# A hybrid attention layer whose residual gate moves from TensorE to VectorE, with the entry of the softmax attention and the planner's costs rewritten

## The chip, the core and the metric

The kernel runs on one core of a Trainium2 chip. The metric is device time in microseconds, the median of several executions; one further execution is recorded by the hardware profiler. A measurement of this kernel can tell a difference of about 0.3% from none.

## What is computed

One layer over 1024 latent tokens and 256 context tokens of width 1024. Two branches read the same modulated input: a bidirectional chunked gated linear attention (GLA, 4 heads) and a differential softmax attention (8 heads, two score maps each). Their outputs are merged and projected, and the residual gate `g_x` scales the result:

```python
mod_x = jax.nn.silu(c) @ w_ada[layer] + b_ada[layer]
sh_x, sc_x, g_x = jnp.split(mod_x[:, None, :], 3, axis=-1)
pl = project(modulate(x, sh_x, sc_x), w_in[layer])
pc = project(modulate(ctx, sh_c, sc_c), w_in[layer])
...
o_gla = bidir_gla(q, k, v, la_f, la_b, s_f, s_b)
...
o_diff = diff_attention(q1, q2, concat(ck1, k1), concat(ck2, k2), concat(cv, dv), lam)
a = merge_heads(rms_norm(o_gla) * gla_gain) * silu(gla_gate)
b = merge_heads(rms_norm(o_diff) * diff_gain * (1 - lam_init)) * silu(diff_gate)
y = sigmoid(m_gla) * (a @ w_br_gla) + sigmoid(m_diff) * (b @ w_br_diff)
x = x + g_x * (y @ w_out[layer])
```

`g_x` is one row of 1024 numbers: the last third of `silu(c) @ w_ada + b_ada`.

## The kernel before

All data are fp32. A product of accuracy near fp32 is made of three one-pass products (`mm3`, L322): each operand is split into a rounded part and a rest (`split`, L332: ScalarE copies, VectorE subtracts).

The program is written as many small generators, and a planner (`Driver`, L57) decides at build time in which order TensorE, ScalarE, VectorE and GpSimd get their instructions. It keeps a clock of its own, with a cost for each instruction (`Engine`, L175, and `mm`, L316) and for each transfer (`Driver.dma`, L118), and at each moment issues what is due, by priority. On the chip the engines do not look at that clock: each takes its instructions strictly in the order so written, and waits where an input is late. So a change of the costs changes the order and nothing else. Transfers all stand in one queue on SP, in order too.

The work goes in three phases.

- Phase A (`phase_a`, L752): fifteen jobs stream slices of `w_in` through three load buffers (tag `raw`), split them (tag `w`), and multiply (PSUM tag `mm`) for keys, values, queries and gates; what later phases need is stored in DRAM (`d_kT`, `d_dv`, `d_qT`, ...). Into the second half of this stream the planner weaves the GLA's four heads (PSUM tags `gs`, `go`, `gt`; `gla_head`, L1046), whose small products depend on one another.
- The residual gate (`job_gate`, L702) is made in phase A. Its slice of `w_ada` is loaded and split like any weight, and 32 products with the two parts of `silu(c)` (`cs`) as stationary operand give two rows of 512 columns twice, which go to DRAM (`d_g`). In phase C `gate` (L1839) loads them back to all partitions and adds bias.
- Phase B (`phase_b`, L1755) is the attention. It begins when the stream and the GLA are both done (`ev_b2`, `ev_b`). `att_keys`, `att_queries` and `att_values` (L1336 to L1370) load the operands (tags `kk`, `aq`, `vv`). For each head and each tile of 128 queries TensorE makes scores (tags `st` for 256 and `s2` for 1024 keys), VectorE the maximum, ScalarE the exponentials, VectorE the difference of the two maps (tag `e5`); TensorE transposes the result in groups of 4, 4 and 2 (`att_tr`, L1466, PSUM tag `b1`), ScalarE copies each group from PSUM (tag `ac`), GpSimd splits it (tags `at4`, `at2`), and for each pair of tiles TensorE multiplies with the values (`att_av`, L1491, also PSUM tag `b1`, of which there are two). `att_fin` (L1548) normalises, with two more transposes from tag `b1k`. Between all this `fill` (L1599) gives TensorE other products (tags `mb`, `wt`), one half tile per 1.3 query tiles.
- Phase C (`phase_c`, L1813): the merge and the output product (tag `mc`).

Of the kernel before, what the change touches and what calls it, by code (L numbers as in the profile page):

```python
# [56 lines left out]
class Driver:  # L57
# [60 lines left out]
    def dma(self, nbytes, dst, src):  # L118
        t = max(self.free["DGE"], self.now, self.ready.get(self.key(src), 0.0)) + 0.6
        self.free["DGE"] = t  # L120
        t = max(self.free["DMA"], t + 0.6) + nbytes / 360e3
        self.free["DMA"] = t
        t += 1.8
        k = self.key(dst)
        self.ready[k] = max(t, self.ready.get(k, 0.0))
        return At(t)
# [48 lines left out]
class Engine:  # L175
# [5 lines left out]
    def __getattr__(self, what):  # L181
        f = getattr(self.eng, what)

        def emit(out, *args, **kw):
# [8 lines left out]
            psum = any(x.space == PSUM for x in ins)  # L193
            if self.name == "ACT":
                c = 0.06 + 0.000833 * n + 0.093 * scalars + (0.0 if psum else 0.04)
            elif self.name == "DVE":
                fast = what in ("tensor_scalar", "tensor_copy") and not psum
                c = 0.07 + n / 960 * (0.5 if fast else 2.0 if "scan" in what else 8.0 if what == "reciprocal" else 1.0)
            elif ALU.pow in args:
                c = 0.3 + 0.165 * n  # L200
            elif what == "tensor_tensor":
                c = 0.15 + 0.0021 * n
            else:
                c = 0.16 + 0.00083 * n + 0.083 * scalars
# [9 lines left out]
class Hybrid:  # L214

    TAGS = dict(
        h=("sb", 32), raw=("sb", 3), sm=("sb", 32),
# [10 lines left out]
        wt=("sbW", 4), ft=("sbW", 2), aq=("sbB2", 4), kk=("sbB2", 3), vv=("sbB2", 3),  # L228
        e5=("sbB", 6), at4=("sbB", 6), at2=("sbB", 2), ac=("sbB", 2), b1k=("sbB", 5), fin=(None, 2),

        yy=("sbC", 32), o=("sbC", 4), gb=("sbC", 1), wx=("sbC", 4),

        mm=("psA", 3), tp=("psA", 2), gs=("psA1", 1), go=("psA1", 1), gt=("psA1", 1),
        mb=("psW", 1), s2=("psB", 2), st=("psB1", 1), b1=("psB1", 2), mc=("psC", 4),
    )
    POOLS = dict(sb="left", sbA="left", sbB="left", sbC="left",
# [99 lines left out]


    def build(self):
        tc = self.tc
        with (  # L340
# [4 lines left out]
            with tc.manual_schedule(engines={ENG.PE, ENG.Activation, ENG.DVE, ENG.Pool}):  # L345
                self.open("sb", "sbA", "psA", "psA1", "sbA1")
# [4 lines left out]
                self.close("psC", "psW", "sbW", "sbC", "sb")  # L351

    def scratch(self):
# [14 lines left out]
        self.d_g = d("d_g", [2, D])  # L368
# [383 lines left out]
    def phase_a(self):  # L752
# [8 lines left out]
        self.ev_st = {(nm, c, i): Event() for nm in ("gg", "dq", "dg") for c in range(2) for i in range(8)}  # L761
# [29 lines left out]
        def stream():  # L791
            for n, j in enumerate(jobs):
# [6 lines left out]
                if n == self.NG:  # L799
                    d.spawn(self.job_gate(), prio=8)  # L800
# [176 lines left out]
    def post_qk(self, isk, c, i, pm):  # L977
# [37 lines left out]
        for j in range(4):  # L1015
# [10 lines left out]
                   ("pl", 2), ev=None if isk else self.ev_st["dq", c, i])  # L1026
# [343 lines left out]
    def att_values(self):  # L1370
        yield self.ev_b2
# [227 lines left out]
    def fill(self):  # L1599
# [8 lines left out]
        yield self.ev_b2  # L1608
# [12 lines left out]
        def conv(n, raw):  # L1621
            tg = wtag(n)
            if tg == "wx":
# [11 lines left out]

        d.spawn(load(), prio=3)
# [274 lines left out]
```

## Time and profile before

| | us |
|---|---|
| median of 3 runs | 1765.09 (1763.59 to 1769.03) |
| the profiled execution, device time | 1769.03 |
| its span in the profile | 1767.3 |
| TensorE busy | 1703.3 (96%) |
| VectorE busy | 1056.0 (60%) |
| ScalarE busy | 761.1 (43%) |
| GpSimd busy | 735.4 (42%) |

The profile gives one execution. A row names an engine, an operation, the tile written and those read (`out<-in`, without numbers), how often it stands there and how long it took. PE is TensorE's matmul, PEld its weight load, DVE is VectorE, ACT is ScalarE, POOL is GpSimd, SP the queue of transfers. The ends of matmuls are modelled, since they overlap: 128x512 matmuls are listed with some 0.4 us each and follow one another faster than that. A number in square brackets behind a row is idle time before it, with what ended it.

### The profile page before, as it was taken

Reading aid. Unit: us, or ns where it says so; the run is one execution under the profiler, and the core shown is the slowest. Engines: PE = TensorE matmul, PEld = TensorE weight load, DVE = VectorE, ACT = ScalarE, POOL = GpSimd, SP = SyncE. Lnnn points to the kernel's source line nnn. Section 1 sums busy time; section 2 is a strip of 40 time slices with the busy share of each in tenths; the row PEclk is TensorE's granted clock in tenths of the full one; section 3 lists DMA queues with packets and bytes.
Section 4 is the critical chain, followed back from the end, with each engine's and each line's share of the span. In section 5 each row is a group of like instructions: output and inputs, shape, how many; then the busy total and the mean of one; then the engine's idle time right before and its main releaser. Section 6 shows DMA issues by size and latency. Waiting matters only on the chain.

```text
span 1767.3 us, 25056 instructions
## 1 busy us (share of the span) xinstructions
PE 1703.3 (96%) x8633; PEld 1400.0 (79%) x8633; DVE 1056.0 (60%) x1895; ACT 761.1 (43%) x1759; POOL 735.4 (42%) x918
## 2 busy tenths in 40 slices
PE   7999999999999999999999999999999898999998
PEld 3788768888888788788788788788887787888887
DVE  4535233615553768878852987777877788535532
ACT  4546342212242444443432666566665555522200
POOL 1500001403333445545530577777876776831000
PEclk9999999999999999999999999999999999999999
DMA  8423352433743545555447344345348553269522
GB/s 310 146 81 133 129 179 90 131 123 118 220 147 113 187 144 171 149 154 168 132 131 190 91 121 124 107 114 133 113 114 251 176 143 96 81 201 303 180 102 84
DMA packets 244903, 259.90 MB, mean 147 GB/s; under 512 B 20860, under 2 KB 176420, under 8 KB 244776
## 3 DMA queue, kind: packets, MB, share of 16 engines
q1 hardware_dynamic: 244776, 258.30, 47.9%
q8 instruction: 68, 1.11, 0.3%
q14 instruction: 59, 0.48, 0.1%
HBM read 171.72 MB, written 86.52 MB: 146 GB/s over the span
## 4 chain that ended last, share of the span: by engine, by line
PE 78%; DVE 12%; ACT 3%; DMA 3%; issue 2%; POOL 2%; SPq 0%; ACTq 0%; DVEq 0%; POOLq 0%
PE mm L317 38%; PE mc L317 12%; PE mb L317 7%; DVE sm L185 6%; PE b L317 4%; PE s L317 4%; PE b L329 3%; PE go L317 3%; PE gs L317 2%; PE st L317 2%; PE tp L329 2%; PE gt L317 2%; DVE e L185 1%; POOL sm L185 1%; DVE b1k L185 1%
## 5 line engine op out<-in xcount | busy, mean ns | idle before, releaser
L317 PE MATMUL mm<-w,h 128*128 128x512 f32 x2304 | 570.6, 399 | 0.9 <-ACT w L185 0.7
L317 PEld LDWEIGHTS mm<-w,h 128*128 128x128 f32 x2304 | 425.7, 188 | 86.9 <-ACT w L185 1.1
L185 POOL TENSOR_TENSOR at<-ac,at 128x512 fp32r<-128x512 f32 (+1 forms) x192 | 237.5, 1237 | 16.0
L317 PE MATMUL mb<-h,wt 128*128 128x512 f32 x792 | 213.7, 406 | 5.6 <-DVE ft L185 5.4
L185 POOL TENSOR_SCALAR sm<-sm 128x1 f32<-128x1 f32 (+1 forms) x78 | 17.8, 228 | 458.1 <-DVE sm L185 343.7
L185 POOL TENSOR_SCALAR at<-ac 128x512 fp32r<-128x512 f32 (+1 forms) x192 | 136.0, 708 | 168.1 <-ACT ac L185 167.3
L185 DVE TENSOR_TENSOR w<-raw,w 128x512 fp32r<-128x512 f32 x136 | 97.6, 737 | 116.7 <-ACT w L185 113.1
L317 PEld LDWEIGHTS mb<-h,wt 128*128 128x128 f32 x792 | 140.2, 189 | 31.5 <-DVE ft L185 6.1
L185 ACT ACTIVATE p<-mm 128x512 f32<-128x512 f32 (+1 forms) x116 | 67.5, 587 | 217.5 <-PE mm L317 199.7
L185 ACT ACTIVATE ac<-b 128x512 f32<-128x512 f32 (+1 forms) x213 | 107.5, 511 | 122.3 <-PE b L329 101.7
L185 DVE TENSOR_REDUCE sm<-s 128x1 f32<-128x1024 f32 x128 | 155.6, 1216 | 2.7 <-PE s L317 1.5
L185 ACT ACTIVATE e<-s,sm 128x1024 f32<-128x1024 f32 x128 | 143.9, 1124 | 0.0
L317 PE MATMUL b<-at,vv 128*128 128x256 f32 x960 | 130.1, 288 | 10.0 <-ACT ac L185 7.2
L317 PE MATMUL mm<-h,w 128*128 128x512 f32 x576 | 139.1, 398 | 0.5 <-DVE h L185 0.4
L317 PEld LDWEIGHTS b<-at,vv 128*128 128x128 f32 x960 | 122.4, 193 | 16.6 <-ACT ac L185 9.8
L317 PE MATMUL s<-kk,aq 128*128 128x512 f32 x512 | 133.6, 398 | 0.3 <-ACT p L185 0.3
L317 PEld LDWEIGHTS mm<-h,w 128*128 128x128 f32 x576 | 108.9, 191 | 25.4 <-DVE h L185 1.1
L185 POOL TENSOR_TENSOR sm<-sm,nhalf 128x1 f32<-128x1 f32 (+2 forms) x110 | 115.7, 1052 | 31.2 <-DVE sm L185 21.9
L317 PEld LDWEIGHTS s<-kk,aq 128*128 128x128 f32 x512 | 91.7, 191 | 15.6 <-ACT p L185 0.5
L185 DVE SCALAR_TENSOR_TENSOR e<-e,sm,e 128x1280 f32<-128x1280 f32 x64 | 102.3, 1598 | 0.1
L185 ACT ACTIVATE w<-raw 128x512 fp32r<-128x512 f32 x136 | 82.0, 625 | 40.6 <-PE mm L317 24.9
L329 PE MATMUL b<-ident,e 128*128 128x128 f32 x604 | 94.0, 277 | 5.0 <-ACT ac L185 4.5
(195 smaller groups left out, 2647.3 us busy)
## 6 DMA issues: line engine op xcount, KB each, us to landing
raw<-in_w_in SPq DMA_DIRECT2D x72, 512.0 KB, 4.2
aq<-d_qT SPq DMA_DIRECT2D x128, 128.0 KB, 3.4
d_kT<-pl SPq DMA_DIRECT2D x40, 256.0 KB, 2.3
d_dv<-pl SPq DMA_DIRECT2D x40, 256.0 KB, 2.2
gv<-d_v SPq DMA_DIRECT2D x40, 256.0 KB, 3.1
kk<-d_kT SPq DMA_DIRECT2D x32, 320.0 KB, 6.3
vv<-d_dv SPq DMA_DIRECT2D x16, 640.0 KB, 6.1
d_aT<-gpl SPq DMA_DIRECT2D x64, 128.0 KB, 2.1
```

What stands on the lines that cost most here:

```text
L185: f(out, *args, **kw)
L317: self.nc.tensor.matmul(out, lhsT, rhs, start=start, stop=stop)
L329: self.nc.tensor.transpose(out, src, self.ident[:n, :n])
```

## The change

Three things.

The gate: `job_gate` loads the slice of `w_ada` in the same pieces, and VectorE multiplies each by the column `silu(c)` per partition and adds up over the eight pieces into `gb`. One product with a matrix of ones then sums over the partitions, for each of the two halves, which leaves the gate on all partitions at once; VectorE adds the bias, GpSimd halves it. The trip through DRAM and `gate` in phase C go away.

The entry of the attention: the buffers of the keys (`kk`) move to a pool that is there from the start, so the first keys load as soon as they have been stored (`ev_st["dk", ...]`). The values wait for the first queries. `fill` loads its first weights after the last of phase A's, not at the end of the GLA.

The planner's costs: new numbers for transfers, ScalarE, VectorE, GpSimd and TensorE. The order of all four engines comes out anew. The buffers of dynamic transfers shrink (`dynamic_dma_scratch_size`), and an unused tile `edge` of 96 bytes sets where the pools begin.

```diff
     def dma(self, nbytes, dst, src):
-        t = max(self.free["DGE"], self.now, self.ready.get(self.key(src), 0.0)) + 0.6
+        t = max(self.free["DGE"], self.now, self.ready.get(self.key(src), 0.0)) + 0.45
...
+            acc = "accum_out" in kw
+            scalars -= acc and n > 1
             if self.name == "ACT":
-                c = 0.06 + 0.000833 * n + 0.093 * scalars + (0.0 if psum else 0.04)
+                c = 0.2 + 0.000833 * n + 0.093 * scalars - (0.028 if psum else 0.0) + (0.21 if acc else 0.0)
             elif self.name == "DVE":
                 fast = what in ("tensor_scalar", "tensor_copy") and not psum
-                c = 0.07 + n / 960 * (0.5 if fast else 2.0 if "scan" in what else 8.0 if what == "reciprocal" else 1.0)
+                c = 0.16 + 0.055 * scalars + n * 0.00104 * (
+                    0.5 if fast else 2.0 if "scan" in what else 8.0 if what == "reciprocal" else 1.0)
...
-        c = (max(n, 256) if rhs.dtype == F32R else 2 * max(2 * n, 256)) / 2400
+        c = 0.009 + max(n, 230) * 0.000428 if rhs.dtype == F32R else 0.006 + max(4 * n, 470) / 2400
...
     def job_gate(self):
         yield self.ev_la
-        wd = self.wstream([(self.a["w_ada"][0], 2048), (self.a["w_ada"][0], 2560)], "w", prio=2)
+        a = self.a
+        gb = self.gb = self.t("gb", [P, 2, 512])
         for n in range(2):
+            o = 2048 + n * 512
+            for kk in range(NK // 2):
+                yield from self.acq("raw")
+                raw = self.t("raw", [P, 2, 512])
+                self.dma(raw, a["w_ada"][0][kk * 256:(kk + 1) * 256, o:o + 512].rearrange("(k p) c -> p k c", p=P))
+                yield self.d.when(raw)
+                for j in range(2):
+                    k = 2 * kk + j
+                    c = self.col[:, k:k + 1]
+                    if k == 0:
+                        e = self.dve.tensor_scalar(gb[:, n], raw[:, j], c, None, ALU.mult)
+                    else:
+                        e = self.dve.scalar_tensor_tensor(gb[:, n], raw[:, j], c, gb[:, n], ALU.mult, ALU.add)
+                    yield e
+                self.rel("raw", e)
+            yield from self.acq("p")
+            bias = self.t("p", [P, 512])
+            self.dma(bias, a["b_ada"][0:1, o:o + 512].to_broadcast([P, 512]))
             yield from self.acq("gs")
-            pm = self.t("gs", [2, 512])
-            for k in range(NK):
-                yield wd[n, k]
-                wh, wl = wd[n, k].w
-
-                prods = [(pm, self.cs[:, k, ::2], wh), (pm[:1], self.cs[:, k, :1], wl)][::-1 if k else 1]
-                for x, (o, c, w) in enumerate(prods):
-                    e = self.mm(o, c, w, k == 0 and x == 0, k == NK - 1 and x == 1)
-                self.rel("w", e, 2)
-                yield AtPE(0)
-            yield from self.acq("p")
-            st = self.t("p", [2, 512])
-            self.rel("gs", self.act.activation(st, pm, AF.Copy))
-            self.store([(self.d_g[:, n * 512:(n + 1) * 512], st)], ("p", 1))
+            pm = self.t("gs", [P, 512])
+            yield self.d.whenpe(gb)
+            e = self.mm(pm, self.ones, gb[:, n], True, True)
+            yield e
+            yield self.d.when(bias)
+            e = self.dve.tensor_tensor(bias, pm, bias, ALU.add)
+            self.rel("gs", e)
+            yield e
+            self.rel("p", self.pool.tensor_scalar(gb[:, n], bias, 0.5, 0.0, ALU.mult, ALU.add))
...
-                    d.spawn(self.job_gate(), prio=8)
+                    d.spawn(self.job_gate(), prio=2)
...
     def att_keys(self):
-        yield self.ev_b2
+
         for hd in range(8):
             c, x = hd // 4, hd % 4
+            for i in range(10):
+                yield self.ev_st["dk", c, i]
+            if hd:
+                yield self.ev_q[0, 1]
...
     def att_values(self):
-        yield self.ev_b2
+        yield self.ev_q[0, 0]
...
-        yield self.ev_b2
...
         def conv(n, raw):
             tg = wtag(n)
+            yield self.ev_b2
...
+        yield self.wload[-1]
         d.spawn(load(), prio=3)
```

How the order moves, at three places. First TensorE where the gate's products stand (tile `gs`, read from `w` and `cs` before). Before:

```order
L317 MATMUL mm_2032<-h_567,w_2002 128x512
L317 MATMUL gs_1784<-w_2074,cs 1x512
L317 MATMUL gs_1784<-w_2073,cs 2x512
L317 MATMUL gs_1784<-w_2090,cs 1x512
L317 MATMUL gs_1784<-w_2089,cs 2x512
L317 MATMUL gs_1784<-w_2094,cs 1x512
L317 MATMUL gs_1784<-w_2093,cs 2x512
L317 MATMUL gs_2118<-w_2099,cs 2x512
L317 MATMUL gs_2118<-w_2100,cs 1x512
```

and now:

```order
L320 MATMUL mm_2139<-h_365,w_1982 128x512
L320 MATMUL mm_2139<-h_366,w_1982 128x512
L320 MATMUL mm_2139<-h_365,w_1983 128x512
L320 MATMUL gs_2152<-gb_1816,ones 128x512
L320 MATMUL mm_2139<-h_562,w_1992 128x512
L320 MATMUL mm_2139<-h_563,w_1992 128x512
```

Of 32 products, of which 22 stood together with nothing between them, two are left, each among the matmuls of a job.

Second, SP at the entry of the attention, behind the last two stores of the GLA (`d_aT`). Before:

```order
L282 DMA d_aT_95<-gpl_8552 128x2x128
L282 DMA d_aT_99<-gpl_8553 128x2x128
L282 DMA d_m_117<-p_8565 128x512
L282 DMA kk_8597<-d_kT_88 64x1280
L282 DMA kk_8597<-d_kT_90 64x1280
...
L282 DMA kk_8603<-d_kT_90 64x1280
L282 DMA vv_8606<-d_dv_82 128x10x128
L282 DMA vv_8608<-d_dv_84 128x10x128
L282 DMA vv_8610<-d_dv_82 128x10x128
L282 DMA aq_8612<-d_qT_86 64x2x256 x2
L282 DMA aq_8615<-d_qT_86 64x2x256 x2
```

and now:

```order
L285 DMA d_aT_95<-gpl_8618 128x2x128
L285 DMA d_aT_99<-gpl_8619 128x2x128
L285 DMA aq_8656<-d_qT_86 64x2x256 x2
L285 DMA aq_8659<-d_qT_86 64x2x256 x2
L285 DMA aq_8662<-d_qT_86 64x2x256 x2
L285 DMA aq_8665<-d_qT_86 64x2x256 x2
L285 DMA raw_8688<-in_w_in 128x8x128
L285 DMA vv_8699<-d_dv_82 128x10x128
```

The keys are gone from here (they stand among the stores of phase A), and the queries come first. On TensorE 150 matmuls of 512 columns stood between the GLA's last transposes and the first score; now 45 do, and the other 105 stand between the steps of the GLA.

Third, TensorE in the eighth head, where the products with the values of one pair of query tiles begin (tile `b` from `at` and `vv`; transposes are `b` from `ident` and `e`, scores `st` and `s`). Before:

```order
L329 MATMUL b_3568_15625<-ident,e_3446_15125 128x128 x4
L317 MATMUL mb_15459<-h_13932,wt_14771 128x512
L317 MATMUL mb_15459<-h_13934,wt_14771 128x512
L317 MATMUL mb_15459<-h_13932,wt_14772 128x512
L329 MATMUL b_3570_15639<-ident,e_3446_15125 128x128 x2
L329 MATMUL b_3577_15656<-ident,e_3460_15190 128x128 x4
L317 MATMUL b_3578_15663<-at_3518_15421,vv_14629 128x256
```

and now:

```order
L332 MATMUL b_3529_15510<-ident,e_3403_14994 128x128 x2
L320 MATMUL mb_15517<-h_13870,wt_14820 128x512
L320 MATMUL mb_15517<-h_13872,wt_14820 128x512
L320 MATMUL mb_15517<-h_13870,wt_14821 128x512
L332 MATMUL b_3534_15523<-ident,e_3431_15104 128x128 x4
L320 MATMUL st_15528<-kk_13856,aq_15243 128x256 x2
L320 MATMUL st_15528<-kk_14773,aq_15246 128x256 x2
L320 MATMUL s_3539_15541<-kk_13856,aq_15243 128x512 x4
L320 MATMUL s_3541_15551<-kk_14773,aq_15246 128x512 x4
L320 MATMUL b_3546_15563<-at_3475_15290,vv_14494 128x256
```

The scores of the next query tile, four products of 256 and eight of 512 columns, now stand between the transposes and the products with the values, and so it is in every second tile of the last three heads.

## Rows read from the trace of the kernel before

**Rows 1.** The page, busy time, share of the span, instructions, by engine.

```profile
PE 1703.3 (96%) x8633; PEld 1400.0 (79%) x8633; DVE 1056.0 (60%) x1895; ACT 761.1 (43%) x1759; POOL 735.4 (42%) x918
```

**Rows 2.** Busy time by stage: stretch, length, each engine (x instructions), TensorE clock, DMA share, GB/s.

```profile
184.00:250.00 66.00, 62.08 (x263) 45.34 (x261) 20.02 (x29) 27.51 (x42) 0.00 (x0) 0.98 0.43 143
476.00:927.00 451.00, 443.71 (x2180) 368.66 (x2179) 314.66 (x672) 181.43 (x472) 202.41 (x314) 1.00 0.51 155
962.00:1010.00 48.00, 45.69 (x245) 37.85 (x246) 41.38 (x69) 30.76 (x78) 18.77 (x22) 1.00 0.21 67
1010.00:1320.00 310.00, 297.50 (x1777) 253.89 (x1776) 243.26 (x430) 197.63 (x517) 236.34 (x257) 0.99 0.46 122
1320.00:1590.00 270.00, 250.87 (x1447) 211.78 (x1446) 176.93 (x307) 136.82 (x352) 180.97 (x203) 0.99 0.51 155
1590.00:1767.00 177.00, 172.68 (x756) 141.66 (x754) 73.43 (x102) 23.64 (x37) 7.33 (x3) 1.00 0.50 168
```

**Rows 3.** Timeline of TensorE at the gate: start, us, operation, count, idle time before.

```profile
232.02 0.62 PE L317 MATMUL gs<-w,cs 128*2 128x512 f32 x2
...
240.94 1.09 PE L317 MATMUL gs<-w,cs 128*2 128x512 f32 x4 [0.93 <-ACT p L185]
243.35 1.23 PE L317 MATMUL gs<-w,cs 128*1 128x512 f32 x4 [1.31 <-DVE w L185]
245.22 1.23 PE L317 MATMUL gs<-w,cs 128*1 128x512 f32 x4 [0.64 <-DVE w L185]
247.44 1.87 PE L317 MATMUL gs<-w,cs 128*1 128x512 f32 x4 [0.99 <-DVE w L185]
249.35 13.02 PE L317 MATMUL mm<-h,w 128*128 128x512 f32 x53
```

**Rows 4.** The chain that ended last, an undisturbed stretch of the stream.

```profile
416.16 5.50 PE mm L317 x24
```

**Rows 5.** Timeline of TensorE, two fp32 products of 256 columns in the GLA.

```profile
918.91 0.60 PE L317 MATMUL go<-gsf,gqe 128*128 128x256 f32 x2
919.35 0.59 PE L317 MATMUL go<-gsb,gqe 128*128 128x256 f32 x2
```

**Rows 6.** Groups of VectorE's instructions by form: count, busy us, mean ns, idle before.

```profile
L185 DVE TENSOR_TENSOR w<-raw,w 128x512 fp32r<-128x512 f32 x136 | 97.6, 737 | 116.7 <-ACT w L185 113.1 <-PE gs L317 2.8
L185 DVE SCALAR_TENSOR_TENSOR p<-p,mm 128x512 f32<-128x512 f32 x32 | 21.7, 684 | 30.1 <-ACT p L185 29.8
```

**Rows 7.** Timeline of TensorE between the end of the GLA and the first score.

```profile
927.06 0.38 PE L329 MATMUL tp<-ident,gp 128*128 128x128 f32 x2
927.20 34.31 PE L317 MATMUL mm<-h,w 128*128 128x512 f32 x150
961.35 0.64 PE L317 MATMUL st<-kk,aq 128*128 128x256 f32 x4
```

**Rows 8.** Timeline of SP's queue in the same stretch.

```profile
929.93 3.83 SPq L282 DMA_DIRECT2D kk<-d_kT  x6
933.80 8.18 SPq L282 DMA_DIRECT2D vv<-d_dv  x3
942.03 7.15 SPq L282 DMA_DIRECT2D aq<-d_qT  x8
```

**Rows 9.** The page's loads: count, KB each, median us from issue to landing.

```profile
aq<-d_qT SPq DMA_DIRECT2D x128, 128.0 KB, 3.4
```

**Rows 10.** Timeline of TensorE in the attention, four of the longest waits.

```profile
1212.85 2.40 PE L317 MATMUL b<-at,vv 128*128 128x256 f32 x18 [1.75 <-ACT ac L185]
1386.65 0.53 PE L329 MATMUL b<-ident,b1k 128*128 128x128 f32 x2 [3.85 <-DVE b1k L185]
1475.13 1.69 PE L317 MATMUL b<-at,vv 128*128 128x256 f32 x12 [1.51 <-ACT ac L185]
1495.44 0.97 PE L317 MATMUL mb<-h,wt 128*128 128x512 f32 x3 [2.85 <-DVE ft L185]
```

More of the change, by code (lines that the diff above doesn't have):

```diff
@@ L216 @@
     TAGS = dict(
-        h=("sb", 32), raw=("sb", 3), sm=("sb", 32),
+        h=("sb", 32), raw=("sb", 3), gb=("sb", 1), sm=("sb", 32), kk=("sb", 3),
         w=("sbA", 18), p=("sbA", 5), pl=("sbA", 4), rope=("sbA", 1),
@@ L226 @@
         gsm=("sbA2", 8),
-        wt=("sbW", 4), ft=("sbW", 2), aq=("sbB2", 4), kk=("sbB2", 3), vv=("sbB2", 3),
+        wt=("sbW", 4), ft=("sbW", 2), aq=("sbB2", 4), vv=("sbB2", 3),
         e5=("sbB", 6), at4=("sbB", 6), at2=("sbB", 2), ac=("sbB", 2), b1k=("sbB", 5), fin=(None, 2),
-        yy=("sbC", 32), o=("sbC", 4), gb=("sbC", 1), wx=("sbC", 4),
-        mm=("psA", 3), tp=("psA", 2), gs=("psA1", 1), go=("psA1", 1), gt=("psA1", 1),
+        yy=("sbC", 32), o=("sbC", 4), wx=("sbC", 4),
+        mm=("psA", 3), tp=("psA", 2), edge=("sbE", 1), gs=("psA1", 1), go=("psA1", 1), gt=("psA1", 1),
         mb=("psW", 1), s2=("psB", 2), st=("psB1", 1), b1=("psB1", 2), mc=("psC", 4),
     )
-    POOLS = dict(sb="left", sbA="left", sbB="left", sbC="left",
+    POOLS = dict(sbE="right", sb="left", sbA="left", sbB="left", sbC="left",
                  sbA1="right", sbA2="right", sbW="right", sbB2="right",
@@ L335, in split @@
         return self.dve.tensor_tensor(lo, src, hi.bitcast(F32), ALU.subtract)
+    EDGE = 96
     def build(self):
@@ L345, in build @@
             with tc.manual_schedule(engines={ENG.PE, ENG.Activation, ENG.DVE, ENG.Pool}):
+                self.open("sbE")
+                self.t("edge", [P, self.EDGE // 4])
                 self.open("sb", "sbA", "psA", "psA1", "sbA1")
@@ L350, in build @@
                 self.d.run()
-                self.close("psC", "psW", "sbW", "sbC", "sb")
+                self.close("psC", "psW", "sbW", "sbC", "sb", "sbE")
     def scratch(self):
@@ L367, in scratch @@
         self.d_y = [d(f"d_y{i}", [P, S]) for i in range(8)]
-        self.d_g = d("d_g", [2, D])
     def consts(self):
@@ L760, in phase_a @@
         self.ev_gla, self.ev_stream = Event(), Event()
-        self.ev_st = {(nm, c, i): Event() for nm in ("gg", "dq", "dg") for c in range(2) for i in range(8)}
+        self.ev_st = {(nm, c, i): Event() for nm in ("gg", "dq", "dg", "dk") for c in range(2)
+                      for i in range(10 if nm == "dk" else 8)}
         allt = list(range(10))
@@ L1025, in post_qk @@
         self.store([(dst[j][:, :, o:o + P].rearrange("h p t -> p h t"), x) for j, x in enumerate((hi, lo))],
-                   ("pl", 2), ev=None if isk else self.ev_st["dq", c, i])
+                   ("pl", 2), ev=self.ev_st["dk" if isk else "dq", c, i])
     def post_gate(self, dif, c, i, pm):
@@ L1826, in to_c @@
             yield self.ev_att
-            yield from self.idle("st", "b1", "e5", "b1k", "aq", "kk", "vv", "at4", "at2", "ac")
+            yield from self.idle("st", "b1", "e5", "b1k", "aq", "vv", "at4", "at2", "ac")
             self.close("psB1", "sbB2", "sbB")
@@ L1832, in to_c @@
             wd = self.wstream([(wo, 0), (wo, 512)], "h")
-            gb = self.t("gb", [P, 2, 512])
-            d.spawn(gate(gb), prio=3)
             yield self.ev_fill
             d.spawn(load_x(), prio=3)
-            d.spawn(stream(wd, gb), prio=9)
-        def gate(gb):
-            yield from self.acq("o", 3)
-            t = [self.t("o", [P, 2, 512]) for _ in range(3)]
-            for x, src in enumerate((self.d_g[0:1], self.d_g[1:2], a["b_ada"][0:1, 2048:3072])):
-                self.dma(t[x], src.rearrange("o (c n) -> o c n", c=2).to_broadcast([P, 2, 512]))
-            yield d.when(*t)
-            yield self.pool.tensor_tensor(t[0], t[0], t[1], ALU.add)
-            yield self.pool.tensor_tensor(t[0], t[0], t[2], ALU.add)
-            self.rel("o", self.pool.tensor_scalar(gb, t[0], 0.5, 0.0, ALU.mult, ALU.add), 3)
+            d.spawn(stream(wd, self.gb), prio=9)
         ev_x = {(c, i): Event() for c in range(2) for i in range(8)}
@@ L1898 @@
     from concourse.bass_utils import run_bass_kernel_spmd
-    nc = bacc.Bacc("TRN2", target_bir_lowering=False, num_devices=1)
+    nc = bacc.Bacc("TRN2", target_bir_lowering=False, num_devices=1, dynamic_dma_scratch_size=1024)
     arrays, aps = {}, {}
```

6 lines of the change are left out of this document (3 added, 3 removed).

## The prediction, made before the changed kernel ran

> **What bounds the kernel now.** I read the page's busy line first. TensorE shows 96% busy [rows 1]; that says only that no long hole is left, since the ends of matmuls are modelled. So I then asked the windows of busy time by stage, and took in each the length less TensorE's busy time as its idle time [rows 2]: 3.9 us of 66 in the stretch with the gate's products, 7.3 of 451 in the linear attention (GLA), 2.3 of 48 just after the entry of the softmax attention, 12.5 of 310 in its regular middle, 19.1 of 270 in its last part, and 4.3 of 177 in the output stage, where the 4.3 are the store after the last matmul. VectorE is busy 243 of the 310 us in the middle and GpSimd 236, so neither is full: TensorE's queue is the bound, and what the others do matters where TensorE, which takes its instructions strictly in order, stands before one whose input is late. The timeline of TensorE shows those places with what ended the wait [rows 3, 10]. In between, matmuls of 512 columns stream: 24 in 5.50 us, 0.229 us each [rows 4].
>
> The sum is made against the profiled execution, 1769.03 us (span 1767.3). It is the slowest of the three runs shown; their median is 1765.09, 3.9 us less, and I subtract that at the end.
>
> **1. The gate: its products leave TensorE.** Before, 32 one-pass products of 512 columns stand on TensorE, 2 (halves) x 8 (k) x 2 (parts). At 0.229 us they stream for 7.3 us. From 240.94 to 249.35 there is nothing else to do, because the weights of the next job wait for the same three load buffers, and TensorE idles 0.93 + 1.31 + 0.64 + 0.99 = 3.9 us between them [rows 3]. Together 11.2 us. What comes is two products of full fp32. The nearest row is the fp32 product of 256 columns in the GLA: one such product is a row of two records, and the next starts 0.44 us behind it [rows 5]. For 512 columns I double it, 0.88 us, so 1.8 us for two. Net -9.4 us. Both orders say that the idle time should not come back: the gate's loads now alternate with those of the weights, and the two products stand among ordinary matmuls (the gate's fence in the section on the change). Bounds: -5.6 if the 3.9 us of idle time return at another place, -11.2 if the two products cost nothing.
>
> VectorE gets 16 passes of 128x512, two additions from PSUM, and loses 16 subtractions of the same shape. The subtraction takes 0.737 us and the nearest form of the new one 0.684 [rows 6], so this is even within 1 to 2 us, in a stretch where VectorE is busy 20 of 66 us [rows 2]. ScalarE loses 16 copies and gains nothing, GpSimd gains two short passes where it did none. All lie beside TensorE's stream; without that cover the 16 passes would cost 11 us (second rival below). The residual gate's three loads and three GpSimd passes at the end go away: TensorE has no idle time but the last store there [rows 2], so I count 0.
>
> **2. The entry of the attention.** The trace shows what the old one costs: after the last transposes of the GLA at 927.06, 150 matmuls stream until the first score at 961.35 [rows 7], and under them SP issues the keys, then the values, then the queries, the last at 949 [rows 8]. TensorE idles 2.3 us in the 48 behind it [rows 2], so there is nearly nothing to win at the entry itself. The new order leaves only 45 matmuls behind the last transposes, 45 x 0.229 = 10.3 us of cover instead of 34.3. The keys no longer belong to what must fit under it, since they are loaded long before. What still has to come behind the GLA: SP got to its first load 2.9 us after the transposes; eight issues of queries took 7.15 us, of which the first scores need four, 3.6 us [rows 8]; a load lands 3.4 us after its issue [rows 9]. That is 9.9 us against 10.3. I take +1 us, bounds 0 and +4 (the same chain with all eight issues ahead of the score, 13.5 us, leaves 3.2 bare).
>
> **3. The GLA.** The same matmuls, but 105 of the 150 that stood behind its end (24 us) now stand between its steps. So more of TensorE's work lies between a step's result and the next step that needs it. TensorE idles 7.3 us there [rows 2]; I take back 4, about half, since the order shows the room but not which waits close it. Bounds 0 and 7.3.
>
> **4. The order of the attention.** The planner's costs are rewritten: PE 512 columns from 0.213 to 0.228 us, which is what the trace shows [rows 4], and longer ones for VectorE and ScalarE. Same instructions, another order. It can win at most what idles, 2.3 + 12.5 + 19.1 = 33.9 us [rows 2]. In the regular middle both orders repeat every head, and the work that TensorE has between the last transposes and the product with the values that needs their PSUM slot is alike (0, 0, 0.7 and 1.4 us before, 0.7, 0, 2.1 and 1.4 now, in matmuls by their durations). There the wait at 1212.85 [rows 10] should stay in one form or another: 2 of the 12.5 us back. In the last part the old order is irregular, and its three worst waits are 3.85, 1.51 and 2.85 us [rows 10]; the new one repeats one pattern every two query tiles, with scores, 2.3 us of work whose inputs lie ready, between transposes and value products (the last fence of the change). I take back 12 of the 19.1. Sum -14, bounds 0 and -34.
>
> **Sum.** 1769.0 - 9.4 + 1 - 4 - 14 = 1742.6; less the 3.9 to the median, 1738.7. Forecast **1739 us**.
>
> **A rule on the clock.** The granted clock is 0.98 of full in the gate's stretch and 0.99 through the attention [rows 2], so of its two levels, 2.4 and 1.2 GHz, the lower one shows only briefly, around places where TensorE had idled; the mean costs 0.02 x 66 + 0.01 x 580 = 7 us. The Trainium skill (TensorE: Matmul & The Clock Gate, HAM oscillation) says that idle gaps between bursts put the array back to half rate. By that rule a new hole at the entry would cost twice, and closing old ones would give up to these 7 us back, 1732 instead of 1739; the row agrees in kind, but no row ties a fall to one of these waits.
>
> **Rivals.**
> - *Forecast:* gate and part of the idle time. 1739, between 1722 and 1752 by the bounds of the terms taken half way. Chance 0.60.
> - *Only the gate counts*, or not even all of it: the new order moves the waits about without removing them, or VectorE's 16 passes stand ahead of weight conversions and give the 11 us back. For: VectorE is half full in the neighbouring jobs, and the middle of the attention looks alike in both orders. Against: the late part clearly changes. 1765.1 - 9.4 + 1 = 1757, or 1765 with the gate's gain lost. Chance 0.22, of it 0.13 for over 0.3% faster, 0.09 for no change.
> - *More than the idle time goes:* short waits that the modelled ends of matmuls hide go too, and the clock stays up. All of the idle time of GLA and attention, 41, the gate's 11 and the 7 us of clock: 1765 - 59 = 1706. For: a matmul is listed as busy beyond the 0.229 us after which the next can start [rows 4], so short gaps behind it don't show as idle time. Chance 0.09.
> - *Slower:* the start of the value products. They need a PSUM slot that ScalarE frees by its copy, and that copy stands behind two exponentials. At 1212.85 this cost 1.75 us [rows 10]. If the new order meets this wait at each of the 32 pairs, it is 56 us where 33.9 are idle now: 1765.1 + 22 - 9.4 - 4 + 1 = 1775. It decides from an average of (33.9 + 12.4) / 32 = 1.45 us a pair on (12.4 being what the other terms win); today all waits of the attention together make 1.06 a pair. For: in each head of the middle one pair still stands directly behind its transposes. Against: before it was two, and in the last three heads none does now. Chance 0.09.
>
> **How the numbers follow.** A measurement of this kernel can tell about 0.3% (5.3 us) from no change. Faster by more, under 1759.8: 0.60 + 0.13 + 0.09 = 0.82; within it 0.09; slower 0.09. The range reaches from 1710, near the large case, to 1762, over the case in which only the gate counts; it leaves out about half of the large case, the slower one, and a little of the second.
>
> **What would show it.** Right: TensorE's instructions fall by 30 products; no wait for a gate product, and the stretch from 184 to 250 loses some 10 us; the first score starts some 12 us earlier than 961, with an idle time of at most 3 us before it; idle time from 1320 to the end of the attention falls under 10 us. Wrong: value products waiting for ScalarE's copies in every pair; a hole of over 4 us before the first score; weight conversions behind the gate's passes on VectorE with TensorE waiting for them.

## The result and the profile after

The changed kernel takes 1735.47 us, the median of 6 runs (1732.79 to 1738.76); the kernel before took 1768.2 us in its 6 runs beside them (1763.59 to 1769.03). The ratio is 0.9822, 95% interval 0.9805 to 0.984: 32.7 us faster. The forecast was 1739. The profiled execution took 1732.79 us (span 1731.1), 36.2 us less than the profiled one of before; the rest of this document divides these 36.2.

The page's busy line of the changed kernel answers to [rows 1]:

```profile
PE 1681.9 (97%) x8605; PEld 1398.8 (81%) x8605; DVE 1036.4 (60%) x1897; ACT 750.7 (43%) x1741; POOL 708.7 (41%) x917
```

As before, the line says only that TensorE sets the pace. The stages say more. The windows below are those of [rows 2], moved to the same places of the program (columns as there):

```profile
182.00:234.00 52.00, 52.00 (x231) 43.08 (x230) 16.27 (x21) 19.18 (x27) 0.00 (x0) 1.00 0.38 137
460.00:926.00 466.00, 465.65 (x2288) 390.23 (x2287) 304.37 (x672) 183.68 (x478) 195.43 (x314) 1.00 0.48 151
936.00:992.00 56.00, 52.67 (x289) 44.02 (x288) 41.99 (x72) 33.59 (x84) 24.82 (x28) 1.00 0.38 112
992.00:1302.00 310.00, 289.29 (x1737) 248.69 (x1736) 241.69 (x424) 195.41 (x509) 229.00 (x255) 0.99 0.44 122
1302.00:1545.00 243.00, 235.20 (x1410) 203.12 (x1409) 165.91 (x307) 135.37 (x350) 169.40 (x199) 1.00 0.51 158
```

Length less TensorE's busy time is 0 around the gate (3.9 before), 0.4 in the GLA (7.3), 3.3 at the entry (2.3), 20.7 in the middle of the attention (12.5) and 7.8 in its late part (19.1). So three stages lost idle time, and the middle got more. (Only the idle times compare, not the lengths: the last window holds 217 output products before and 177 now.)

**Lengths instead of idle time.** Idle time in a window leaves out short waits that lie under the modelled end of a matmul. So I also took the starts of the same TensorE instructions in both traces, and the distance between them. "Gate" runs from the 801st to the 1,201st product of the projections (tile `mm`), "GLA" from the 2,001st to the last of them, "hole" from there to the first score, "heads 1-6" from the first score to that of the seventh head, and "rest" from there to the start of the last output product. A row is one execution, the profiled one; the medians, in the second column, lie up to 3.8 us off it (gate_and_entry: 1753.06 against 1749.24). Differences under a microsecond mean little: the gate's stretch takes 107.2 to 108.5 in the four kernels that leave it as it was. All in us:

| kernel | median | up to the gate | gate | between | GLA | hole | heads 1-6 | rest |
|---|---|---|---|---|---|---|---|---|
| before | 1768.2 | 228.3 | 107.9 | 201.7 | 423.3 | 0.2 | 408.8 | 392.1 |
| changed | 1735.5 | 225.9 | 95.4 | 200.7 | 413.8 | 0.2 | 417.0 | 373.3 |
| gate_only | 1754.2 | 229.5 | 95.6 | 201.7 | 423.6 | 0.2 | 408.5 | 391.4 |
| entry_only | 1762.5 | 227.7 | 107.2 | 200.6 | 423.5 | 0.2 | 407.4 | 390.1 |
| costs_only | 1768.2 | 228.3 | 107.2 | 201.8 | 413.8 | 11.8 | 418.2 | 376.6 |
| gate_and_costs | 1754.8 | 228.3 | 95.5 | 201.8 | 413.7 | 11.3 | 421.6 | 375.3 |
| entry_and_costs | 1748.5 | 228.9 | 108.5 | 200.7 | 413.8 | 0.2 | 418.1 | 373.3 |
| gate_and_entry | 1749.2 | 227.6 | 95.4 | 200.6 | 423.4 | 0.2 | 408.7 | 390.8 |
| without_PE_cost | 1758.1 | 231.9 | 95.4 | 200.7 | 421.9 | 0.2 | 434.4 | 367.2 |
| PE_cost_only | 1768.9 | 228.4 | 96.2 | 200.6 | 426.6 | 0.2 | 418.2 | 392.0 |
| no_fill_loads | 1739.8 | 228.3 | 95.5 | 201.8 | 413.7 | 0.2 | 414.5 | 376.9 |
| all_costs_scaled | 1735.5 | 225.4 | 95.3 | 200.7 | 418.3 | 0.2 | 407.1 | 380.4 |
| shorter_latency | 1731.7 | 228.7 | 95.4 | 200.7 | 416.9 | 0.2 | 405.5 | 379.7 |
| values_first | 1738.0 | 226.8 | 95.4 | 200.7 | 413.8 | 2.4 | 417.4 | 372.9 |

The first two rows divide the gain: gate 12.5, GLA 9.5, attention and output 10.6 (8.2 lost in the first six heads, 18.8 won after them), between gate and GLA 1.0, and 2.4 ahead of the gate. These last 2.4 I don't count as the change's: kernels with much the same order there (entry_and_costs, values_first) stand at 228.9 and 226.8.

**The gate.** Timeline of TensorE in the changed kernel, where [rows 3] showed the old products (start, us, operation, count):

```profile
239.73 9.01 PE L320 MATMUL mm<-h,w 128*128 128x512 f32 x39
248.58 1.02 PE L320 MATMUL gs<-gb,ones 128*128 128x512 f32 x2
249.04 3.30 PE L320 MATMUL mm<-h,w 128*128 128x512 f32 x12
```

The first of the two products with ones (the profile lists a product of full fp32 as two records) stands in an unbroken stream, in place of the 32 products and their four idle times. The second stands the same way, at 296.68.

**The entry.** TensorE's timeline, then that of SP's queue, from the GLA's last transposes on; they answer to [rows 7] and [rows 8]:

```profile
925.61 0.38 PE L332 MATMUL tp<-ident,gp 128*128 128x128 f32 x2
925.75 10.50 PE L320 MATMUL mm<-h,w 128*128 128x512 f32 x45
936.08 0.63 PE L320 MATMUL st<-kk,aq 128*128 128x256 f32 x4
```

```profile
926.48 0.91 SPq L285 DMA_DIRECT2D d_aT<-gpl  x2
927.44 5.11 SPq L285 DMA_DIRECT2D aq<-d_qT  x8
932.65 0.54 SPq L285 DMA_DIRECT2D raw<-in_w_in  x1
933.28 4.69 SPq L285 DMA_DIRECT2D vv<-d_dv  x3
```

Forty-five products of cover are left, as the order said, and the queries are loaded first under them (then a weight of `fill`, then the values): the first score follows without a hole.

**GLA and attention.** What TensorE waited for (us in total, times, longest), first in the GLA of the kernel before, from 476 to 927 us:

```profile
PE tp L329 <- DVE gp L185: 3.8, 5, 1.5
PE gt L317 <- ACT gkt L185: 1.9, 2, 1.4
```

In the changed kernel's GLA the first is gone and the second is 0.2 us, the longest there. In the middle of the attention, 1010 to 1320 us in the kernel before:

```profile
PE b L317 <- ACT ac L185: 5.7, 4, 1.7
PE b L329 <- DVE b1k L185: 3.7, 7, 0.9
PE b L317 <- DVE b1k L185: 1.9, 4, 0.5
```

and in the changed kernel, 992 to 1302:

```profile
PE b L332 <- DVE b1k L185: 8.4, 11, 1.3
PE b L332 <- ACT ac L185: 7.8, 9, 1.5
PE b L320 <- ACT ac L185: 3.1, 3, 1.0
```

and in its late part, 1302 to 1545, where the waits of 3.85 and 2.85 us of [rows 10] have no successor:

```profile
PE b L332 <- ACT ac L185: 4.2, 5, 1.3
PE b L332 <- DVE b1k L185: 2.2, 5, 1.1
```

The waits of the value products (L317, now L320) moved to the transposes (L329, now L332). By the tiles that they read, 7.8 of the 7.8 us and 8.2 of the 8.4 us in the middle stand before transposes of the exponentials: these and the value products take the same two PSUM slots (tag `b1`), which copies on other engines free.

### The profile page after: what moved, and what is told of

Read it like the earlier page. It is cut to its first block, busy times and chain, and to the rows that moved or that the text cites. A ratio compares the mean times of both kernels' runs of the same rounds, so it can differ in the third digit from the quotient of the medians.

```text
span 1731.1 us, 25030 instructions
## 1 busy us (share of the span) xinstructions
PE 1681.9 (97%) x8605; PEld 1398.8 (81%) x8605; DVE 1036.4 (60%) x1897; ACT 750.7 (43%) x1741; POOL 708.7 (41%) x917
## 4 chain that ended last, share of the span: by engine, by line
PE 87%; DVE 5%; DMA 2%; ACT 2%; issue 2%; POOL 2%; SPq 0%; ACTq 0%; DVEq 0%; POOLq 0%
PE mm L320 42%; PE mc L320 12%; PE mb L320 7%; PE b L320 6%; PE s L320 5%; PE b L332 3%; DVE sm L185 3%; PE go L320 3%; PE gs L320 2%; PE gt L320 2%; PE tp L332 2%; PE st L320 2%; POOL at L185 1%; DMA w<-in_w_ada 1%; DVE e L185 1%
## 5 line engine op out<-in xcount | busy, mean ns | idle before, releaser
L320 PE MATMUL mm<-w,h 128*128 128x512 f32 x2304 | 569.3, 399 | 1.4 <-DVE w L185 1.4
L320 PEld LDWEIGHTS mm<-w,h 128*128 128x128 f32 x2304 | 425.6, 188 | 87.5 <-DVE w L185 2.1
L185 POOL TENSOR_TENSOR at<-ac,at 128x512 fp32r<-128x512 f32 (+1 forms) x192 | 222.1, 1157 | 16.0
L320 PE MATMUL mb<-h,wt 128*128 128x512 f32 x792 | 218.1, 405 | 1.2 <-ACT ft L185 0.7
L185 POOL TENSOR_SCALAR at<-ac 128x512 fp32r<-128x512 f32 (+1 forms) x192 | 145.2, 756 | 143.1 <-ACT ac L185 131.1
L320 PEld LDWEIGHTS mb<-h,wt 128*128 128x128 f32 x792 | 138.8, 189 | 25.0 <-DVE ft L185 1.5
L185 ACT ACTIVATE ac<-b 128x512 f32<-128x512 f32 (+1 forms) x213 | 107.9, 508 | 103.4 <-PE b L332 82.7
L320 PE MATMUL mm<-h,w 128*128 128x512 f32 x576 | 143.3, 401 | 0.7 <-DVE h L185 0.6
L320 PE MATMUL s<-kk,aq 128*128 128x512 f32 x512 | 134.9, 397 | 0.2 <-ACT p L185 0.2
L320 PE MATMUL b<-at,vv 128*128 128x256 f32 x960 | 131.8, 287 | 3.1 <-ACT ac L185 3.1
L320 PEld LDWEIGHTS b<-at,vv 128*128 128x128 f32 x960 | 124.1, 192 | 7.4 <-ACT ac L185 3.9
L320 PEld LDWEIGHTS mm<-h,w 128*128 128x128 f32 x576 | 107.9, 191 | 24.1 <-DVE h L185 1.6
L185 DVE TENSOR_TENSOR w<-raw,w 128x512 fp32r<-128x512 f32 x120 | 86.3, 736 | 64.4 <-ACT w L185 63.1
L332 PE MATMUL b<-ident,e 128*128 128x128 f32 x604 | 94.2, 275 | 23.8 <-ACT ac L185 12.7
L185 POOL TENSOR_TENSOR sm<-sm,nhalf 128x1 f32<-128x1 f32 (+2 forms) x110 | 107.2, 975 | 13.9 <-DVE sm L185 7.4
L332 PEld LDWEIGHTS b<-ident,e 128*128 128x128 f32 x604 | 71.5, 140 | 44.8 <-ACT ac L185 18.7
L320 PEld LDWEIGHTS s<-kk,aq 128*128 128x128 f32 x512 | 90.8, 190 | 14.8 <-ACT p L185 0.4
```

What stands on the lines that cost most here:

```text
L185: f(out, *args, **kw)
L332: self.nc.tensor.transpose(out, src, self.ident[:n, :n])
```

## The experiments

Each kernel ran beside the kernel before; its median then was 1766.96 us with the first four, 1766.94 with the next four, 1764.05 with the three after them, and 1766.26 with the last.

**gate_only.** `job_gate` as in the change, with the smaller buffers of dynamic transfers (as in every kernel here but costs_only); costs and entry as before. One of its lines:

```diff
-                    d.spawn(self.job_gate(), prio=8)
+                    d.spawn(self.job_gate(), prio=2)
```

> The gate's part alone (job_gate on VectorE, its priority 2, gb in the pool sb; the small DMA scratch is kept because gb does not fit without it); planner's costs and the attention's entry as before. Theory that the parts add (P): the gate is worth 13.5 us, all of it between the matmuls that stand at 228 and 265 us in the kernel before, so about 1754.5 us (1751 to 1758), with GLA and the attention at the same lengths as before. Rival A (the forecast's own size): 9.4 us, 1758.6. Rival J (the parts only work together, because each new order of the attention is a new draw): anything from 1735 to 1775, and the difference lies outside the gate's stretch.

1754.22 us, ratio 0.9926 (0.9905 to 0.9948): 12.7 us. The table puts 12.3 us between the two gate marks, and elsewhere only 1.2 ahead of the gate, the other way, and less than a microsecond in each column behind it. The gate is a part by itself.

**entry_only.** The pools, keys, values, fill's loads and the edge tile, nothing else of the change's three parts; for example:

```diff
-        yield self.ev_b2
+        yield self.ev_q[0, 0]
```

> The entry's part alone (kk in the pool sb, keys' loads by their own events, values after the first queries, fill's loads early, the edge tile, the small DMA scratch); gate and costs as before. P: the entry by itself brings nothing that lasts, 1768 us plus or minus 4. Rival E (the entry is what shortens GLA's end and the way to the first score): 1768 less 9 to 10, about 1758, with the first score some 10 us earlier than 961. Forecast's term: 1 us slower.

1762.5 us, ratio 0.9974 (0.9963 to 0.9986): 4.5 us: a little more than P allows (4), and under half of E's 9 to 10, whose place is wrong as well, since the GLA and the first score's distance behind it are unchanged. Of the gain, 3.5 lie in the attention and 1.1 between gate and GLA; the 1.1 come with every kernel that has the edge tile and fill's early loads, and with none that lacks them (200.6 or 200.7 against 201.7 or 201.8).

**costs_only.** The planner's numbers alone, for example

```diff
-        c = (max(n, 256) if rhs.dtype == F32R else 2 * max(2 * n, 256)) / 2400
+        c = 0.009 + max(n, 230) * 0.000428 if rhs.dtype == F32R else 0.006 + max(4 * n, 470) / 2400
```

> The planner's new costs alone (PE, ACT, DVE, POOL and DMA); gate and entry as before. P: the rest of the gain, 36 - 13.5 = some 20 us, about 1747 us (1742 to 1754), from GLA (about 9) and the attention from the fourth head on (some 20), less some 10 in the first heads if that loss belongs to the order. Rival E: 1757 or more, since GLA's part is the entry's. Rival J: no gain, 1762 to 1774.

1768.15 us, ratio 1.0008 (0.9995 to 1.0021): nothing, as J said and P did not. The table shows why, in part: the GLA is 9.5 us shorter and the rest 15.5, and against them stand 9.4 in the first six heads and a hole of 11.8 us before the first score. (These parts leave a gain of 4 us that the medians don't have: the profiled execution, 1764.55, is the fastest of ten, and that of before the slowest of its six.) The loss in the first heads is of the kind that J meant; the hole is not. TensorE's timeline there (in brackets the idle time before a row and what ended it):

```profile
944.73 6.74 PE L320 MATMUL mm<-h,w 128*128 128x512 f32 x29
962.92 0.76 PE L320 MATMUL st<-kk,aq 128*128 128x256 f32 x2 [11.46 <-DMA aq<-d_qT]
964.02 0.77 PE L320 MATMUL st<-kk,aq 128*128 128x256 f32 x2 [0.33 <-DMA aq<-d_qT]
964.59 3.20 PE L320 MATMUL s<-kk,aq 128*128 128x512 f32 x8
967.63 4.61 PE L320 MATMUL mb<-h,wt 128*128 128x512 f32 x19
```

and SP's queue in the same kernel:

```profile
942.66 4.64 SPq L285 DMA_DIRECT2D kk<-d_kT  x6
947.35 7.81 SPq L285 DMA_DIRECT2D vv<-d_dv  x3
955.20 7.21 SPq L285 DMA_DIRECT2D aq<-d_qT  x8
```

Keys, values and queries all wait for the GLA's buffers and take 19.8 us of issue; of the 34 us of products that used to cover them [rows 7] the new order has left 10.5, 45 products from 940.96 on, of which the first row above shows the last 29.

**gate_and_costs.** Both together:

> Gate and costs together, entry as before (small DMA scratch kept). P: 1768 - 13.5 - 20, about 1734.5 us, as the whole change. If the loss of 10 us in the first two heads is the entry's doing, 1725. Rival E: 1744 or more. Rival J: 1740 to 1770.

1754.78 us, ratio 0.9932 (0.9911 to 0.9954): the gate's 12.2 and again nothing from the costs, with the same hole (11.3). P fell here; "entry and costs need each other" took its place.

**entry_and_costs** leaves the gate's part out of the change, **gate_and_entry** leaves the costs out:

> The whole change without the gate's part. By the first four runs the gate is worth 12.5 us wherever it stands, the costs alone 0, the entry alone 4.5. Theory that entry and costs need each other (N: the costs put more of the projections under GLA and end them 10 us earlier, but open a hole of 11.5 us before the first score, since the loads of kk, vv and aq follow GLA's end; the entry's part takes that hole away): 1735.5 + 12.7 = 1748 us (1745 to 1752), idle before the first score under 1 us. Rival (the gate is what the order needed, GC): 1762, the sum of the two parts alone.

> The whole change with the planner's costs as before. N: 1767 - 12.7 - 4.5 = 1750 us (1746 to 1753); first score some 13 us earlier than 961, late attention as in the kernel before. Rival (the costs matter little once gate and entry are in): 1740 or less.

1748.54 us (0.9895, 0.9878 to 0.9911) and 1749.24 us (0.9901, 0.9884 to 0.9918), each within 1 us of what N gave. With the entry's part the costs bring 14 us more (1762.5 to 1748.5), without it nothing. In gate_and_entry TensorE's timeline has the old cover again:

```profile
913.05 34.27 PE L317 MATMUL mm<-h,w 128*128 128x512 f32 x150
```

**without_PE_cost** and **PE_cost_only** split the costs. The first keeps the old line for `mm` above, the second changes that line alone:

> The whole change, but the planner's cost of a matrix product as before (0.213 us for 512 columns); the new costs of ScalarE, VectorE, GpSimd and DMA stay. If the gain of the order comes from the right matmul cost: 1750, as with all costs old. If it comes from the costs of the three other engines: 1736 to 1739. If each order is a draw of its own: anywhere in 1730 to 1760, with differences in several stages.

> The whole change, but of the planner's costs only that of a matrix product is new; those of ScalarE, VectorE, GpSimd and DMA as before. The mirror of the run before: 1736 to 1739 if the matmul's cost carries the order's gain, 1750 if the other engines' costs do, anywhere in 1730 to 1760 if each order is a draw.

1758.09 us (0.9948, 0.9933 to 0.9963) and 1768.88 us (1.0013, 1.0001 to 1.0025). Either half is worse than both whole tables beside the same gate and entry, old (1749.2) and new (1735.5): no half carries the gain. With the PE cost old, the first six heads take 434.4 us, and the transposes wait for ScalarE's copies all through the attention (its waits from 1010 to 1560 us):

```profile
PE b L332 <- ACT ac L185: 21.1, 22, 2.0
```

With the PE cost alone new, 192 projections are left behind the GLA's end, more than the 150 of before, and the GLA is the longest of all (426.6):

```profile
908.50 43.68 PE L317 MATMUL mm<-h,w 128*128 128x512 f32 x192
```

**no_fill_loads** takes two pieces of the entry back, fill's early loads and the edge tile; of the first:

```diff
+        yield self.ev_b2
...
-        yield self.wload[-1]
```

> The whole change without two pieces of the entry: fill's weight loads wait for the attention's buffers as before, and the edge tile is gone; kk in the pool sb with loads by their own events, and the queries ahead of the values, stay. Theory (keys and queue order are what closes the hole before the first score): idle before the first score under 1 us, 1735.5 plus up to 3 for fill's first products, 1735 to 1739. Rival (fill's early loads are what PE runs on while the attention starts, and without them the hole or a wait of like size comes back): 1745 to 1752.

1739.76 us, ratio 0.9859 (0.9839 to 0.9878): the hole stays closed (0.2), so fill's loads are not what closes it. The median is 4.3 us over that of the change, and the intervals of the two ratios just touch, so these pieces are worth a few us at most, 1.1 of them between gate and GLA.

**all_costs_scaled** keeps the new ratios but shrinks all costs, except DMA's:

```diff
+        cost = cost * 0.934
         t = self.now if eng == "PE" else self.free[eng]
```

> The whole change with the planner's costs of all products and operations times 0.934, which puts a product of 512 columns back at 0.213 us but keeps its ratio to the three other engines; latencies, lead and DMA costs stay. If the ratio of the engines is what the order needs (a wrong PE cost alone gave 1758, wrong costs of the others alone 1769): 1736 to 1742. If the tables must be right in themselves, or each order is a draw: 1748 to 1760.

1735.54 us, ratio 0.985 (0.982 to 0.988). A product costs 0.213 us in the plan again, as in without_PE_cost, yet the time is some 20 us better (22.5 by the medians, 17 by the ratios). So it is the ratio between the engines that the order needs, as far as one factor can show it.

**shorter_latency** brings one more constant near the trace:

```diff
-    LAT = dict(PE=0.24, ACT=0.15, DVE=0.15, POOL=0.15)
+    LAT = dict(PE=0.24, ACT=0.09, DVE=0.09, POOL=0.09)
```

> The whole change with the planner's latency from ScalarE, VectorE and GpSimd to a reader at 0.09 us in place of 0.15; the trace of the changed kernel shows 0.086 us in most cases from a ScalarE copy's end to the GpSimd operation on it. If a truer table always gives a better order: 1735.5 or less. If the orders are draws round a level that the table's errors set: 1735.5 plus or minus 8, with the first heads, the late attention and GLA differing in both directions. If the 0.15 is needed as slack: 1745 or more, with more waits of transposes in every head.

1731.7 us, ratio 0.9815 (0.9797 to 0.9832). It has the lowest median of all, but its interval overlaps that of the change (0.9805 to 0.984): no difference that these runs can tell. In the stages it does differ, in both directions: heads 1-6 are 11.5 us shorter, the GLA 3.1 and the rest 6.4 longer. So the single stages move by some 10 us from order to order, while the sums of the three tables with costs of all engines in proportion lie within 4 us by their medians (6 by their ratios).

**values_first** puts the values ahead of the queries again:

```diff
-        yield self.ev_q[0, 0]
+        yield self.ev_b2
```

> The whole change, but the values' loads wait for the attention's buffers as in the kernel before and not for the first queries, so that vv stands ahead of aq on SP's queue again (kk stays early in the pool sb). With the costs alone the three loads stood between 942.7 and 962.4 us: kk 4.6 us, vv 7.8, aq 7.2 of issue, and the hole before the first score was 11.5. If the queue order is what closes the hole: vv's 5 to 8 us of issue come back as idle before the first score, so about 1735.5 + 5 = 1741 us, at most 1744. If the early kk alone closes it, because TensorE still has projections to run: 1735.5, idle under 1 us.

1738.02 us, ratio 0.9851 (0.9828 to 0.9873), an interval that overlaps that of the change: the time tells nothing, the trace does. A hole comes back, of 2.4 us rather than 5:

```profile
939.08 0.47 PE L320 MATMUL st<-kk,aq 128*128 128x256 f32 x2 [1.97 <-DMA aq<-d_qT]
940.13 0.47 PE L320 MATMUL st<-kk,aq 128*128 128x256 f32 x2 [0.58 <-DMA aq<-d_qT]
940.45 2.00 PE L320 MATMUL s<-kk,aq 128*128 128x512 f32 x8
942.29 4.01 PE L320 MATMUL mb<-h,wt 128*128 128x512 f32 x17
```

```profile
928.32 3.44 SPq L285 DMA_DIRECT2D vv<-d_dv  x3
931.81 6.64 SPq L285 DMA_DIRECT2D aq<-d_qT  x8
```

Of the 11.8 us of hole in costs_only, 9.4 are closed with the keys out of the way (their 4.6 us of issue are gone from there, and that of the values is 4.4 shorter) and 2.2 by the order of the queue. That it is not the gate's part or fill's early loads, which values_first has too, follows from gate_and_costs (a hole of 11.3) and no_fill_loads (0.2).

## Why the prediction was right, and where it was not

The total came 3.5 us below the forecast, inside its range, and its signs held: 30 products fewer (28 records), no wait for a gate product, the stretch at the gate shorter by over 10 us, no hole, late idle time under 10. (The range of the first rival is a slip: half way to the bounds as given lie 1726 and 1751, not 1722 and 1752.) The first score came 25.3 us earlier, not 12. By its terms:

- **Gate, -9.4 forecast, -12.5 measured** (gate_only: 12.7). The mechanism was right, the size too small, and -11.2 was no bound. Summed from each start to the next, the 32 products held TensorE for 13.2 us, not 7.3 + 3.9. The step that failed is the waiting. The 3.9 us of idle time count from the modelled end of a product, 0.39 us behind its start, though the next can start after 0.229. From start to start, less 0.229, the same four waits come to 4.5 us, and two that were too short to be listed to 0.3. Another 1.0 lies in the last four products, which take 0.39 to 0.67 us each to the next start, under a lower granted clock; with the 7.3 that makes 13.1. Windows of the kernel before (columns as in [rows 2]):

```profile
236.00:246.00 10.00, 7.12 (x29) 2.47 (x27) 5.87 (x9) 5.71 (x10) 0.00 (x0) 1.00 0.76 247
246.00:250.00 4.00, 2.97 (x8) 0.79 (x6) 1.97 (x4) 2.49 (x5) 0.00 (x0) 0.68 0.86 250
250.00:252.00 2.00, 2.00 (x9) 1.61 (x8) 1.31 (x3) 1.19 (x3) 0.00 (x0) 0.78 0.91 253
```

  The clock is not what made the gate dear, though. In entry_only, with the same 32 products, it stayed up:

```profile
246.00:250.00 4.00, 2.72 (x10) 1.03 (x10) 2.39 (x4) 1.93 (x4) 0.00 (x0) 1.00 0.81 227
250.00:252.00 2.00, 2.00 (x11) 1.63 (x10) 0.69 (x1) 1.12 (x2) 0.00 (x0) 1.00 0.86 236
```

  and they held TensorE for 13.1 us all the same, waiting more instead (5.3 us from start to start), in a stretch of 107.2 us against 107.9. Behind the last gate product the others take 0.8 us more in the kernel before than the same ones in gate_only. The two fp32 products cost 1.8 us, as forecast: 0.46 and 0.92 us to the next group's start, and the product behind the first takes 0.63 us instead of 0.23. Sum: 13.2 + 0.8 - 1.8 = 12.2, which is 12.5 within the scatter of the stretch.

- **Entry, +1 forecast, 0 measured before the first score** (the whole part by itself gained 4.5, behind that place for the most part). The chain of 9.9 us against 10.3 of cover held: in values_first the queries' issue begins 5.3 us after the last transposes, not 1.8, and 2.2 us are bare, so the change has some 1.3 to spare. What the prediction lacked is what the entry is worth beside the new order: I compared it with the old entry under the old 34 us of cover. Without it the costs open a hole of over 11 us.

- **GLA, -4 forecast, -9.5 measured.** "More work between a step and the next" was right, since costs_only has the whole 9.5. The step that failed is the bound: idle time by windows, 7.3, was taken for all there was to win. The same products take 9.5 us less from first start to last. Less what each kind takes when it streams (the fastest quarter of its steps), the waits before the transposes of `gp` fell from 6.6 to 0.8, and those before the products of tile `gt` by some 4. How much waiting there was in all depends on what one calls streaming (10 us before by the median of a kind's steps, 46 by their fastest quarter): the distances measure what was won, and give a bound only roughly. The third rival named this (short waits under modelled ends), and I gave it to the rival instead of to the term.

- **Order of the attention, -14 forecast, -10.6 measured**, 1.4 of it in gate_and_entry, the rest with the costs. The middle was to give 2; the first six heads took 8.2 instead, of which some 3 are work done earlier (by the seventh head's first score 9 more fill products and 10 more transposes have run). The late part was to give 12 and gave 11.3 by idle time; from the seventh head to the last output product the length fell by 18.8, the same 3 us among them. The failed step is that both orders' middles were called alike: idle time grew there, from 0.7 to 1.2 us a pair (20.7 us over some 17 pairs), nearly all of it now (19.1 us) a wait for a PSUM slot as in the fourth rival, but 16.0 of it before transposes and not before value products, and 8.2 ended by VectorE. Over the whole attention all idle time stays at 1.0 a pair (3.3 + 20.7 + 7.8 over 32 pairs), under the 1.45 from which that rival decides. By idle time alone the attention would have won 2 us (33.9 to 31.8); the length fell by 10.6.

- **The clock rule.** In costs_only the idle 11.46 us were followed by the lower level:

```profile
951.00:963.00 12.00, 0.54 (x4) 0.15 (x2) 1.23 (x1) 2.91 (x4) 0.00 (x0) 0.60 1.16 257
963.00:967.00 4.00, 3.67 (x10) 2.92 (x11) 1.16 (x2) 0.00 (x0) 0.00 (x0) 0.50 1.03 270
967.00:971.00 4.00, 4.00 (x18) 3.17 (x18) 3.35 (x5) 2.96 (x7) 0.00 (x0) 0.98 0.32 95
```

  0.50 is 1.2 of 2.4 GHz. The scores from the first to the next group take 4.71 us there (962.92 to 967.63) and 3.21 in values_first (939.08 to 942.29), where the granted clock stayed at 1.00 after 1.97 us of idle time. By the Trainium skill (TensorE: Matmul & The Clock Gate, HAM oscillation) idle gaps between bursts put the array back to half rate; the 11.46 us of idle time agree, and the 1.97 us show that not every gap does. "A hole costs twice" was wrong in size: this one cost 1.5 us on top of its 11.5. In the gate's stretch the clock's part of the 12.5 is at most 1.8 us by single products (1.0 + 0.8), and 0.7 by the length beside entry_only.

That the forecast came so close is in part luck. Two terms were too small (gate 3.1, GLA 5.5) and the attention's too large (3.4). In all the terms gave 26.4 us, where the two profiled executions lie 36.2 apart: 9.8 short. Of these only 3.2 are left between forecast and median, since the profiled execution of before was the slowest of its runs (3.9 us were taken off for that) and that of after the fastest (2.7 us under its median).

What stays open: why either half of the cost table gives a worse order than the old one. The runs show where (GLA's end, the transposes' waits), not which choice of the planner turns. That the ratio of the costs decides rests on three orders with all costs in proportion (1732 to 1736 us) against the two halves (1758 and 1769) and the old table (1749); that orders are partly draws, as the stages in shorter_latency suggest, is not excluded by so few.

## What to carry to other kernels

Before a change takes work off a place, ask which loads that work was hiding: here the better order alone gained nothing, since it used up the cover of the next stage's loads, and those loads moved ahead alone gained 4.5 us, while both together gained 18. When a planner is given measured costs, give it all engines' costs at once; half a correction was worse than none. And size a gain by the distance from start to start of the same instructions, not by the idle time of a window: the gate's term and the GLA's, both bounded by idle time, came out above their bounds (12.5 over 11.2 and 9.5 over 7.3).

## What the runs showed that I had not expected

The time that a load's issue takes on SP's queue changed with the order: three loads of values took 7.81 us of issue in costs_only, 4.69 in the changed kernel and 3.44 in values_first. And the edge tile's 24 words a partition are worth 1.1 us between gate and GLA. In the changed kernel and in no_fill_loads all engines and SP's queue have the same order in that stretch, and fill's first load comes long after it (932.6 us); yet the 192 products that read tile `hc` take 44.2 us with the tile and 45.4 without (0.227 and 0.234 us from start to start at the median), while every other kind takes the same within 0.1 us. So it is the tile, which moves the pools on its side of SBUF, that of `hc` among them; why that matters to the products, no run shows.
